# Pair blocks with both halves of the activations in one matmul, an earlier pool product and another block order in a two-layer decoder trunk

## The chip, the cores and the metric

The kernel runs on one core of one Trainium2 chip. The metric is the device time of one execution in microseconds (us), as the median of several runs. The kernel before takes 931.28 us (three runs, 930.87 to 931.46). The profile shows one execution on the same core.

## The reference, cut to what matters

Two layers are applied to a sequence of 256 tokens of width 1024, in float32. Each layer is a feed-forward, a mixer with three parallel head groups, and a second feed-forward; every sub-layer stands between two RMS norms.

```python
for l in range(2):
    f = swiglu(rmsnorm(h, ff1_norm_pre[l]), ff1_w_gate[l], ff1_w_up[l], ff1_w_down[l])   # 1024 -> 2816 -> 1024
    h = h + 0.5 * rmsnorm(f, ff1_norm_post[l])
    m = concat([ssd, pool, attention](rmsnorm(h, mix_norm_pre[l]) @ w_in[l])) @ w_out[l]
    h = h + rmsnorm(m, mix_norm_post[l])
    f = swiglu(rmsnorm(h, ff2_norm_pre[l]), ff2_w_gate[l], ff2_w_up[l], ff2_w_down[l])
    h = h + 0.5 * rmsnorm(f, ff2_norm_post[l])
# swiglu(h, wg, wu, wd) = (silu(h @ wg) * (h @ wu)) @ wd
# pool: per group of 64 columns, (sliding mean of u - u) @ pool_w[g], times pool_scale
```

## The kernel before

**Numbers in two parts.** Every operand of a large product is split into a high part `hi`, which ScalarE rounds to the matmul's reduced float32 format, and a remainder `lo` = x - hi, which VectorE forms. A product is then hi·hi + hi·lo + lo·hi, three matmuls. The weights are split on the chip, as they arrive: class `Weights` (L49) loads a unit of 128 x 2048 numbers (1 MB) on the SyncE queue into one of four raw buffers, and `split_next` (L88) makes a job of it, of which at most five are held split at a time. `pump` (L116) loads and splits as far ahead as those buffers allow. The ScalarE rounding is L104, the VectorE remainder L105, and L103 is a sum or difference of two raw units that is wanted as a weight.

**A feed-forward** (`ffn`, L521) cuts the 2816 inner columns into eleven blocks of 256. The first two (`ffn_first`, L422) are computed as soon as the normed input is turned. Of the other nine, the list `QUADS` = 2, 5, 8 names where a *seven* begins and `PAIRS` = 4, 7, 10 the *pairs*:

- A seven (`ffn_quad`, L473) makes two neighbouring blocks, gate and up, for all tokens with seven products of half sizes in place of eight, by sums of the four weight units g1, u1, u2, g2 (jobs g1, T1, T2, T3, g2, T4, u2; each is `product`, L463, 12 matmuls of 512 columns). Its result is the two tiles `h0`, `h1`, which are finished by VectorE after the last products (L512 for h1, L515 for h0).
- A pair (`ffn_pair`, L449) makes one block's gate and its up with `mm_feat` (L313): for each of two groups of 128 output columns, 24 matmuls, where the weight is the stationary operand and 256 tokens of `xT` stream: 8 of hi·x_hi, 8 of hi·x_lo, 8 of lo·x_hi. The two groups share one PSUM bank; gate and up have a bank each. L417 takes the Silu from PSUM, L419 multiplies.

After a seven, its `h0` and `h1` have to be turned by eight transposes (`turn_h`, L446) before its down products. The next block calls that as `turn()`: a pair between its gate and its up (L456), a seven behind its first product (L481). The down products (`mm_rows`, L358) go to four `acc` banks, two for each half of the tokens (t = 0, 1), 12 matmuls for a block and half. Those of the last four blocks are done for t = 0 first, so that the closing norm of t = 0 (`post`, L239) and the opening norm of the next sub-layer (`pre_scale`, L255, whose last step is L260) run on ScalarE, VectorE and GpSimd while TensorE still works for t = 1. Then `pre_turn` (L263) turns the normed tile by transposes, L270.

**The mixer** (`mixer`, L614) ends with: the attention's product (`attend`), the second gate product `zed(1)`, the two scans (`scan`, L926) and the carry between them (L917), the pool product (L967, two matmuls on VectorE's `d`) with its scaling and split (`rows_out`, L869, L219, L220), and the output product: units wa, wp, ws0, ws1 of `w_out` through `mm_rows`, again into two acc banks for each half of the tokens. wa needs the attention, wp the pool, ws0 and ws1 the gated scan after its norm, which `gated_turn` (L944) turns. At the end of t = 1's ws1, `joint` puts the `pre_turn` of the t = 0 half between its two banks.

**Order.** The five engines run what the tile framework's scheduler made of the program; `tc.issue_after` lets a stretch be placed behind a named instruction. The order of each engine is fixed when the program is built. Four `wk` banks and four `acc` banks of PSUM are handed out in turn.

Of the kernel before, what the change touches and what calls it, by code (L numbers as in the profile page):

```python
# [11 lines left out]
F32R = mybir.dt.float32r  # L12
BF16 = mybir.dt.bfloat16
AF = mybir.ActivationFunctionType
ALU = mybir.AluOpType
AX = mybir.AxisListType

P = 128
D = 1024
S = 256  # L20
NT = S // P
DEPTH = 2
KD = D // P
# [6 lines left out]
UNIT = 2048  # L30
# [2 lines left out]
SPLIT_BUFS = 5  # L33
TAIL = 4

FIRST, QUADS, PAIRS = (0, 1), (2, 5, 8), (4, 7, 10)


C_ID, C_U, C_SGT, C_NEG, C_CNT, C_CS = 0, 128, 256, 384, 512, 1024
# [101 lines left out]
def hybrid_trunk_kernel(ctx: ExitStack, tc: tile.TileContext, a, out: bass.AP):  # L141
# [16 lines left out]
    def bank(tag="wk"):  # L158
        return psum.tile([P, 512], F32, tag=tag, name=f"{tag}{next(ids)}")
# [47 lines left out]
        nc.scalar.activation(neg_b, cst[:, C_NEG : C_NEG + P], AF.Copy)  # L207

    gains = consts.tile([P, 2, D], F32, name="gains")
    xT = [consts.tile([P, KD, S], F32R, name=f"xT{i}") for i in range(2)]  # L210

    def load_gain(which, l, n):
        row = a["gains"][l, n : n + 1, :]
# [99 lines left out]
    def mm_feat(ps, u, c, x=xT, ncols=256):  # L313

        hi, lo = (w[:, : KD * ncols].rearrange("p (k n) -> p k n", k=KD) for w in W.get(u))
        s = slice(c, c + P)
        for i, (w, y) in enumerate(((hi, x[0]), (hi, x[1]), (lo, x[0]))):
            for k in range(KD):
                nc.tensor.matmul(ps, w[:, k, s], y[:, k, :], start=i == 0 and k == 0, stop=i == 2 and k == KD - 1)  # L319

    def mm_tok(ps, u, t, ncols=256):

        hi, lo = (w[:, : KD * ncols].rearrange("p (k n) -> p k n", k=KD) for w in W.get(u))
        s = slice(t * P, (t + 1) * P)
        for i, (x, w) in enumerate(((xT[0], hi), (xT[0], lo), (xT[1], hi))):
            for k in range(KD):
                nc.tensor.matmul(ps, x[:, k, s], w[:, k, :], start=i == 0 and k == 0, stop=i == 2 and k == KD - 1)  # L327
# [41 lines left out]
    def plan_ffn(l, n):  # L369


        p = {}

        def down(i):
            p["d", i] = W.plan(a[f"ff{n}_d"][l, i])

        def pair(i):
            for k in "gu":
                p[k, i] = W.plan(a[f"ff{n}_{k}"][l, PAIRS.index(i)])

        for i in range(2):
            for k in range(2):
                p["f", i, k] = W.plan(a[f"ff{n}_f"][l, 2 * i + k], pieces=4)
        before = list(FIRST)
        for i in range(2, NU):
            if i in PAIRS:
                pair(i)
                for b in before:
                    down(b)
                before = [i]  # L390
            elif i in QUADS:
                src = a[f"ff{n}_q"][l, QUADS.index(i)]
                g1, u1, u2 = (W.unit(src[k]) for k in (0, 1, 3))
                p["g1", i] = W.job(g1, pieces=2 if i > QUADS[0] else 4)
                p["T1", i] = W.job(g1, (g1, ALU.add, u1), then=(u1, src[3]))
                p["T2", i] = W.job(g1, (g1, ALU.add, u2))
                late = i == QUADS[-1]
                if not late:
                    down(before[0])
                p["T3", i] = W.job(u1, free=(u1,))  # L400
                g2 = W.unit(src[2])
                p["g2", i] = W.job(g2)
                for b in before[1:]:
                    down(b)
                p["T4", i] = W.job(g1, (g1, ALU.add, g2), free=(g1, g2))
                p["u2", i] = W.job(u2, free=(u2,))
                if late:
                    down(before[0])
                before = [i, i + 1]
        for b in before:  # L410
            down(b)
        return p

    def gate(pg, pu, s=None):
        if s is None:
            s = buf()
            nc.scalar.activation(s, pg, AF.Silu)  # L417
        hf = buf()
        nc.vector.tensor_tensor(hf, pu, s, op=ALU.mult)  # L419
        return hf  # L420
# [26 lines left out]
            split_into(hT[i], (slice(None), slice(None)), ps)  # L447

    def ffn_pair(i, p, turn):  # L449
        pg, pu = bank(), bank()  # L450
        for ps, k in ((pg, "g"), (pu, "u")):
            for j in range(2):
                mm_feat(ps[:, j * 256 : (j + 1) * 256], p[k, i], j * P)
            W.done(p[k, i])
            if k == "g":
                turn()  # L456
        hf = gate(pg, pu)
        hT = (buf(F32R), buf(F32R))
        split_into(hT, (slice(None), slice(None)), hf)
        W.pump()  # L460
        return hT
# [8 lines left out]
                             skip_group_check=not first)  # L470
        W.done(job)

    def ffn_quad(i, p, left, turn, downs):  # L473


        late = i == QUADS[-1]
        pa = bank()
        product(pa, left["X11"], p["g1", i], True)
        w2 = buf()
        nc.scalar.activation(w2, pa, AF.Copy)  # L480
        turn()  # L481
        pc = bank()
        product(pc, left["S1"], p["T1", i], True)
        h1 = buf()
        nc.scalar.activation(h1, pc, AF.Copy)
        if "rest" in left:
            with tc.issue_after(split_into.last.ins):
                left.pop("rest")()
                W.pump()
        else:  # L490
            W.pump()
        pb = bank()
        product(pb, left["S2"], p["T2", i], True)
        nc.vector.tensor_tensor(w2, pb, w2, op=ALU.add)
        nc.vector.tensor_tensor(pc, pc, w2, op=ALU.subtract)
        W.pump()
        if not late:
            downs[0]()
        pd = bank()
        product(pd, left["S3"], p["T3", i], True)  # L500
        nc.vector.tensor_tensor(pd, pd, w2, op=ALU.add)
        nc.vector.tensor_tensor(h1, h1, pd, op=ALU.subtract)  # L502
        W.pump()
        product(pa, left["X12"], p["g2", i], False)
        h0 = buf()
        nc.scalar.activation(h0, pa, AF.Silu)
        W.pump()
        for f in downs[1:]:
            f()
        product(pd, left["X22"], p["T4", i], False)  # L510
        nc.scalar.activation(w2, pd, AF.Silu)
        nc.vector.tensor_tensor(h1, h1, w2, op=ALU.mult)  # L512
        W.pump()
        product(pc, left["S4"], p["u2", i], False)
        nc.vector.tensor_tensor(h0, pc, h0, op=ALU.mult)  # L515
        W.pump()
        if late:
            downs[0]()
        return [h0, h1]

    def ffn(l, n, p, gain, turned, left, next_left, before_next, last, later=None):  # L521
# [19 lines left out]
                W.pump()  # L541

        before = list(FIRST)
        for i in range(2, NU):
            if i not in QUADS + PAIRS:
                continue
            if hf:
                for b in before:
                    hT[b] = (buf(F32R), buf(F32R))

            def turn():
                if hf:
                    turn_h(hf, [hT[b] for b in before])

            if i in PAIRS:
                hT[i] = ffn_pair(i, p, turn)
                for b in before:
                    both(b)
                hf, before = None, [i]
            else:  # L560
                hf = ffn_quad(i, p, left, turn, [lambda b=b: both(b) for b in before])
                before = [i, i + 1]
            if later and i in PAIRS:
                later()
                later = None
# [48 lines left out]
    def mixer(l, p, turned, next_left, before_next):  # L614
# [341 lines left out]
        with tc.issue_after(turn_x.last.ins):  # L956
            sz1 = zed(1)
        with tc.issue_after(zed.last.ins):
            y0 = scan(0)
            yn0 = gated(0, y0, sz0)  # L960
            carry()
            y1 = scan(1)

            pp = bank("acc")
            pw = vec[:, V_PW : V_PW + 256].rearrange("p (j n) -> p j n", j=2)
            for j in range(2):
                m = nc.tensor.matmul(pp[:, j * 256 : (j + 1) * 256], pw[:, j, :], d[:, j, :], start=True, stop=True)  # L967
            y_pool = rows_out(pp, vec[:, V_PS : V_PS + 2])
            yn1 = gated(1, y1, sz1)
        acc = [banks2(), banks2()]  # L970
        with tc.issue_after(m.ins):
            mm_rows(acc[0], p["wa"], 0, y_attn, True, False)
        m = mm_rows(acc[0], p["wp"], 0, y_pool, False, False)
        with tc.issue_after(m.ins):
# [112 lines left out]
def _layout(inp):  # L1087
# [16 lines left out]

        return x.reshape(DEPTH, 2, 4, P, 512).transpose(0, 1, 3, 2, 4).reshape(DEPTH, 2, P, UNIT)

    def quads(g, u):


        q = []  # L1110
        for i in QUADS:
            for h in range(2):
                for w in (g, u):
                    x = w[:, h * 512 : (h + 1) * 512, i * 256 : i * 256 + 512]
                    q.append(x.reshape(DEPTH, 4, P, 512).transpose(0, 2, 1, 3).reshape(DEPTH, P, UNIT))
        return np.stack(q, axis=1).reshape(DEPTH, len(QUADS), 4, P, UNIT)

    for n in (1, 2):
        g, u = f[f"ff{n}_w_gate"], f[f"ff{n}_w_up"]
        d[f"ff{n}_f"] = np.concatenate([half(g[:, :, :512]), half(u[:, :, :512])], axis=1)  # L1120
        d[f"ff{n}_g"] = cols(g)[:, PAIRS]
        d[f"ff{n}_u"] = cols(u)[:, PAIRS]
        d[f"ff{n}_q"] = quads(g, u)
        d[f"ff{n}_d"] = rows(f[f"ff{n}_w_down"])
    w = f["w_in"]
    z, x, B, C, dt, u, q, k, v = np.split(w, np.cumsum([512, 512, 256, 256, 8, 256, 256, 256]), axis=2)
# [37 lines left out]
```

## Time and profile before

| | |
|---|---|
| median of three runs | 931.28 us |
| profiled execution, its own time | 931.69 us |
| its span, from the first to the last instruction | 930.0 us |
| mean granted TensorE clock | 0.997 |
| TensorE matmul busy | 917.9 us, 99% |
| VectorE busy | 785.5 us, 84% |
| ScalarE busy | 584.2 us, 63% |
| first feed-forward, mixer, second feed-forward of layer 0 | about 0 to 189, 189 to 291, 291 to 467 us |

PE is TensorE's matmul, PEld its weight load, DVE VectorE, ACT ScalarE, POOL GpSimd, SP SyncE. A row of the timeline reads: start in us, duration in us, engine, line, operation, output <- inputs by the program's names, shape, count; in brackets the idle time ahead of it on its engine and what ended that. Rows with a count cover consecutive instructions, which overlap a little in their pipelines; the time of one in a run is the distance of starts over the count.

### The profile page before, as it was taken

What the parts mean: (1) busy time and instruction counts of PE and PEld (TensorE: products, weight loads), DVE (VectorE), ACT (ScalarE), POOL (GpSimd) and SP (SyncE); (2) the same over time, 40 slices, a digit from 0 to 9 for tenths busy, and PEclk for the clock granted to TensorE, in tenths of its full rate; (3) what the DMA queues carried; (4) which work ended last, traced back from release to release, by engine and by line L of the source; (5) the groups of instructions that cost most, each with busy time, mean ns of one, the idle gap of its engine ahead of it and who ended that gap; (6) DMA issues with size and microseconds to landing.
All of it is one profiled execution on the core that took longest, in us unless ns stands there. A gap on an engine that the chain in (4) does not pass through costs nothing.

```text
span 930.0 us, 13066 instructions
## 1 busy us (share of the span) xinstructions
PE 917.9 (99%) x5058; PEld 794.0 (85%) x5058; DVE 785.5 (84%) x1019; ACT 584.2 (63%) x931; POOL 30.1 (3%) x49
## 2 busy tenths in 40 slices
PE   7999999999999999999999999999999999999997
PEld 5889898989988888888888988898998888989895
DVE  6999999589868998988599989876989699989872
ACT  7665747478738665646566756556794567656641
POOL 0000000000001000000000000000000110000000
PEclk9999999999999999999999999999999999999999
DMA  8576958465434486848455968583834246868521
GB/s 325 153 274 201 386 157 314 179 215 194 181 109 173 103 304 190 318 135 305 148 181 156 342 171 289 165 315 110 297 104 172 72 145 185 319 203 270 188 101 45
DMA packets 28002, 190.54 MB, mean 205 GB/s; under 512 B 3106, under 2 KB 3362, under 8 KB 5924
## 3 DMA queue, kind: packets, MB, share of 16 engines
q1 hardware_dynamic: 26068, 176.87, 52.1%
q0 software_dynamic: 1728, 12.58, 7.5%
q8 instruction: 39, 0.64, 0.3%
q10 hardware_dynamic: 144, 0.26, 0.1%
q14 instruction: 23, 0.19, 0.1%
HBM read 188.65 MB, written 1.05 MB: 204 GB/s over the span
## 4 chain that ended last, share of the span: by engine, by line
PE 95%; issue 1%; DVE 1%; DMA 1%; ACT 1%; POOL 0%; DVEq 0%; POOLq 0%; SPq 0%; ACTq 0%
PE acc L358 29%; PE wk L469 25%; PE wk L319 21%; PE wk L340 14%; PE wk L446 2%; PE wk L327 1%; PE wk L270 1%; DMA raw<-in_ff_f 1%; DVE lo L105 0%; PE acc L677 0%; PE acc L747 0%; ACT hi L104 0%; ACT n L227 0%; PE acc L879 0%; PE wk L905 0%
## 5 line engine op out<-in xcount | busy, mean ns | idle before, releaser
L104 ACT ACTIVATE hi<-raw 128x1024 fp32r<-128x1024 f32 (+2 forms) x452 | 401.1, 938 | 176.9 <-DVE raw L103 44.6
L105 DVE TENSOR_TENSOR lo<-raw,hi 128x1024 fp32r<-128x1024 f32 (+2 forms) x452 | 467.1, 1079 | 51.5 <-ACT hi L104 50.2
L358 PE MATMUL acc<-hi,t 128*128 128x512 f32 x832 | 216.2, 391 | 0.5 <-DVE t L896 0.5
L358 PEld LDWEIGHTS acc<-hi,t 128*128 128x128 f32 x832 | 154.8, 188 | 32.7 <-DVE t L896 1.4
L319 PE MATMUL wk<-xT,hi 128*128 128x256 f32 x1088 | 143.4, 284 | 0.0
L319 PEld LDWEIGHTS wk<-xT,hi 128*128 128x128 f32 x1088 | 136.7, 191 | 1.7
L358 PE MATMUL acc<-lo,t 128*128 128x512 f32 x416 | 114.1, 390 | 0.0
L469 PE MATMUL wk<-hi,n 128*128 128x512 f32 x384 | 102.9, 390 | 0.0
L340 PE MATMUL wk<-hi,xT 128*128 128x512 f32 x384 | 99.0, 395 | 2.6 <-ACT hi L104 2.6
L358 PEld LDWEIGHTS acc<-lo,t 128*128 128x128 f32 x416 | 78.0, 188 | 16.2
L103 DVE TENSOR_TENSOR raw<-raw,raw 128x1024 f32<-128x1024 f32 x72 | 86.2, 1219 | 1.9 <-DMA raw<-in_ff_q 1.9
L340 PEld LDWEIGHTS wk<-hi,xT 128*128 128x128 f32 x384 | 71.6, 189 | 17.6 <-ACT hi L104 3.4
L469 PEld LDWEIGHTS wk<-hi,n 128*128 128x128 f32 x384 | 71.8, 188 | 14.7
L469 PE MATMUL wk<-hi,xT 128*128 128x512 f32 x288 | 77.8, 392 | 0.0
L319 PE MATMUL wk<-xT,lo 128*128 128x256 f32 x544 | 76.8, 283 | 0.0
L319 PEld LDWEIGHTS wk<-xT,lo 128*128 128x128 f32 x544 | 70.3, 192 | 0.0
L469 PEld LDWEIGHTS wk<-hi,xT 128*128 128x128 f32 x288 | 53.5, 188 | 12.6 <-DVE t L502 1.8
L340 PE MATMUL wk<-lo,xT 128*128 128x512 f32 x192 | 52.3, 395 | 0.0
L469 PE MATMUL wk<-lo,n 128*128 128x512 f32 x192 | 51.3, 389 | 0.0
L244 DVE TENSOR_TENSOR n<-acc,gains 128x512 f32<-128x512 f32 x24 | 16.1, 689 | 33.6 <-ACT n L227 33.6
L340 PEld LDWEIGHTS wk<-lo,xT 128*128 128x128 f32 x192 | 36.6, 191 | 7.8
L469 PEld LDWEIGHTS wk<-lo,n 128*128 128x128 f32 x192 | 36.0, 188 | 7.5
(175 smaller groups left out, 731.2 us busy)
## 6 DMA issues: line engine op xcount, KB each, us to landing
raw<-in_ff_q SPq DMA_DIRECT2D x48, 1024.0 KB, 5.0
raw<-in_ff_d SPq DMA_DIRECT2D x44, 1024.0 KB, 5.0
raw<-in_ff_f SPq DMA_DIRECT2D x16, 1024.0 KB, 6.2
raw<-in_ff_q POOLq DMA_DIRECT2D x12, 1024.0 KB, 8.0
raw<-in_ff_g SPq DMA_DIRECT2D x12, 1024.0 KB, 4.8
raw<-in_ff_u SPq DMA_DIRECT2D x12, 1024.0 KB, 4.9
raw<-in_w_in SPq DMA_DIRECT2D x10, 1024.0 KB, 4.8
raw<-in_w_kvz SPq DMA_DIRECT2D x8, 1024.0 KB, 5.0
```

What stands on the lines that cost most here:

```text
L103: nc.vector.tensor_tensor(raw[:, s], self.raw[x][:, s], self.raw[y][:, s], op=op)
L104: self.act = nc.scalar.activation(hi[:, s], raw[:, s], AF.Copy)
L105: nc.vector.tensor_tensor(lo[:, s], raw[:, s], hi[:, s].bitcast(F32), op=ALU.subtract)
L244: nc.vector.tensor_tensor(fg[i], f[i], gains[:, 1, i * 512 : (i + 1) * 512], op=ALU.mult)
L270: pre_turn.last = nc.tensor.transpose(ps[:, k * P : (k + 1) * P], xn[i][:, k * P : (k + 1) * P], ident)
L319: nc.tensor.matmul(ps, w[:, k, s], y[:, k, :], start=i == 0 and k == 0, stop=i == 2 and k == KD - 1)
L327: nc.tensor.matmul(ps, x[:, k, s], w[:, k, :], start=i == 0 and k == 0, stop=i == 2 and k == KD - 1)
L340: m = nc.tensor.matmul(ps, y[:, k, :], w[:, k, :], start=h == 0 and n == 0, stop=h == 1 and n == len(parts) - 1)
L358: m = nc.tensor.matmul(acc[b], x[:, j, s], w[:, j, b * 512 : (b + 1) * 512], start=first and j == 0 and i == 0, stop=last and j == 1 and i ...
L446: nc.tensor.transpose(ps[:, j * S + t * P : j * S + (t + 1) * P], hf[t][:, c], ident)
L469: nc.tensor.matmul(ps, x[:, k, :], w[:, k, :], start=first and n == 0, stop=n == len(parts) - 1, skip_group_check=not first)
```

## The change

Three edits stand together.

1. **Pairs side by side.** The two halves of the activations, `xT[0]` (high) and `xT[1]` (low), become the two halves of one tile `both`. A new `mm_side` streams x_hi and x_lo in one matmul of 512 columns against the high weight (8 for each group of 128 output columns), then 8 of 256 columns for lo·x_hi into the bank's second half. Each group has a bank of its own, and its two halves have to be added: ScalarE copies one half out, VectorE adds the other. `ffn_pair` takes its Silu and its product from SBUF.
2. **Pool product first.** In the mixer the pool product and its `rows_out` move ahead of the scans, and the wa product now follows the second scan.
3. **Order of the first feed-forward.** For layer 0, n = 1 alone, the sevens are blocks 3, 5, 8 and the pairs 2, 7, 10: pair, seven, seven, pair, seven, pair, where it was seven, pair, seven, pair, seven, pair. The weights are laid out for it on the host. `later`, which loads the constants, two gains and the mixer's parameters, is called behind the first pair, so now behind the first of these blocks instead of the second.

```diff
-FIRST, QUADS, PAIRS = (0, 1), (2, 5, 8), (4, 7, 10)
+FIRST = (0, 1)
+def blocks(l, n):
+    return ((3, 5, 8), (2, 7, 10)) if (l, n) == (0, 1) else ((2, 5, 8), (4, 7, 10))
...
-    xT = [consts.tile([P, KD, S], F32R, name=f"xT{i}") for i in range(2)]
+    both = consts.tile([P, 2, KD, S], F32R, name="xT")
+    xT = [both[:, i] for i in range(2)]
...
+    def mm_side(u, out):
+        hi, lo = (w[:, :UNIT].rearrange("p (k n) -> p k n", k=KD) for w in W.get(u))
+        for j in range(2):
+            s = slice(j * P, (j + 1) * P)
+            ps = bank()
+            for k in range(KD):
+                nc.tensor.matmul(ps, hi[:, k, s], both[:, :, k, :], start=k == 0, stop=k == KD - 1)
+            for k in range(KD):
+                nc.tensor.matmul(ps[:, S:], lo[:, k, s], xT[0][:, k, :], start=False, stop=k == KD - 1,
+                                 skip_group_check=True)
+            o = out[:, j * S : (j + 1) * S]
+            nc.scalar.activation(o, ps[:, S:], AF.Copy)
+            nc.vector.tensor_tensor(o, ps[:, :S], o, op=ALU.add)
+        W.done(u)
+        return out
...
     def ffn_pair(i, p, turn):
-        pg, pu = bank(), bank()
-        for ps, k in ((pg, "g"), (pu, "u")):
-            for j in range(2):
-                mm_feat(ps[:, j * 256 : (j + 1) * 256], p[k, i], j * P)
-            W.done(p[k, i])
-            if k == "g":
-                turn()
-        hf = gate(pg, pu)
+        s = mm_side(p["g", i], buf())
+        nc.scalar.activation(s, s, AF.Silu)
+        turn()
+        hf = mm_side(p["u", i], buf())
+        nc.vector.tensor_tensor(hf, hf, s, op=ALU.mult)
...
         with tc.issue_after(zed.last.ins):
+            pp = bank("acc")
+            pw = vec[:, V_PW : V_PW + 256].rearrange("p (j n) -> p j n", j=2)
+            for j in range(2):
+                pooled = nc.tensor.matmul(pp[:, j * 256 : (j + 1) * 256], pw[:, j, :], d[:, j, :], start=True, stop=True)
+            y_pool = rows_out(pp, vec[:, V_PS : V_PS + 2])
+        with tc.issue_after(pooled.ins):
             y0 = scan(0)
             yn0 = gated(0, y0, sz0)
             carry()
             y1 = scan(1)
-
-            pp = bank("acc")
...
             yn1 = gated(1, y1, sz1)
         acc = [banks2(), banks2()]
-        with tc.issue_after(m.ins):
+        with tc.issue_after(scan.last.ins):
             mm_rows(acc[0], p["wa"], 0, y_attn, True, False)
```

**What moves on the engines: TensorE where the first feed-forward's first seven ends.** The program before: the seven's last product (`wk_425`), then the pair's gate (`wk_656`), and behind that the transposes of `t_569` (h0) and `t_438` (h1).

```order
L469 MATMUL wk_425<-hi_526,n_446 128x512 x4
L319 MATMUL wk_656<-xT_108,hi_549 128x256 x5
L469 MATMUL wk_534<-hi_486,xT_108 128x512 x4
...
L319 MATMUL wk_656<-xT_108,lo_550 128x256 x8
L446 MATMUL wk_706<-ident,t_569 128x128
L446 MATMUL wk_706<-ident,t_438 128x128
```

The program after: the seven's last three jobs end with `wk_610`; then comes the next seven's first product (`wk_798`), and then the transposes of `t_741` (h0) and `t_623` (h1).

```order
L492 MATMUL wk_610<-hi_667,n_631 128x512 x4
L492 MATMUL wk_798<-hi_699,xT 128x512 x4
L492 MATMUL wk_798<-lo_700,xT 128x512 x4
L492 MATMUL wk_798<-hi_699,xT 128x512 x4
L472 MATMUL wk_813<-ident,t_741 128x128
L472 MATMUL wk_813<-ident,t_623 128x128
```

A pair's gate of 48 matmuls stood between the two; now one product of 12 does.

**VectorE at the same place.** L110 are the sums for a seven's jobs, L112 the remainders, L534 finishes h1, L537 makes h0 (`t_741`). The program before first (its L103, L105, L512, L515 are the same steps), then the program after.

```order
L105 TENSOR_TENSOR lo_550<-raw_469,hi_549 128x1024
L105 TENSOR_TENSOR lo_572<-raw_494,hi_571 128x1024 x2
L105 TENSOR_TENSOR lo_604<-raw_496,hi_603 128x1024 x2
L512 TENSOR_TENSOR t_438<-t_438,t_409 128x512
L515 TENSOR_TENSOR t_569<-wk_425,t_569 128x512
```

In the program after, `hi_720` and `hi_743` are the next seven's jobs T1 and T2, and `hi_765` is a down unit.

```order
L110 TENSOR_TENSOR raw_583<-raw_583,raw_648 128x1024 x2
L112 TENSOR_TENSOR lo_721<-raw_583,hi_720 128x1024 x2
L110 TENSOR_TENSOR raw_583<-raw_583,raw_650 128x1024 x2
L534 TENSOR_TENSOR t_623<-t_623,t_608 128x512
L112 TENSOR_TENSOR lo_744<-raw_583,hi_743 128x1024
L112 TENSOR_TENSOR lo_766<-raw_673,hi_765 128x1024
L112 TENSOR_TENSOR lo_744<-raw_583,hi_743 128x1024
L112 TENSOR_TENSOR lo_766<-raw_673,hi_765 128x1024
L537 TENSOR_TENSOR t_741<-wk_610,t_741 128x512
```

So the next seven's T1 and T2 and a down unit are prepared ahead of h0. On ScalarE, `hi_720` stands directly behind the Silu of the g2 product.

**TensorE where the mixer ends its t = 0 half.** The program before: the last matmul of t = 0 (`acc_2653`), the turn of the second gated half (`wk_2713`), t = 1's matmuls (`acc_2654`, `acc_2655`), and the transposes of the next sub-layer's input (`wk_2798`).

```order
L358 MATMUL acc_2653<-hi_2576,t_2470 128x512 x2
L944 MATMUL wk_2713<-ident,t_2650 128x128 x4
L358 MATMUL acc_2655<-lo_2296,t_2525 128x512
...
L358 MATMUL acc_2654<-hi_2576,t_2470 128x512 x2
L270 MATMUL wk_2798<-ident,n_2752 128x128 x4
```

The program after, with `acc_2586` for t = 0, `acc_2587` and `acc_2588` for t = 1:

```order
L383 MATMUL acc_2586<-hi_2509,t_2403 128x512 x2
L967 MATMUL wk_2646<-ident,t_2583 128x128 x4
L383 MATMUL acc_2588<-hi_2333,t_2533 128x512
...
L383 MATMUL acc_2587<-hi_2509,t_2403 128x512 x2
L278 MATMUL wk_2731<-ident,n_2685 128x128 x4
```

Between the turn of the gated half and the transposes of the input stood 35 matmuls of 512 columns; now 21 do, in both layers. The other 14, of wa and wp for t = 1, have moved ahead of ws0 for t = 0.

More of the change, by code (lines that the diff above doesn't have):

```diff
@@ L372, in plan_ffn @@
         p = {}
+        QUADS, PAIRS = blocks(l, n)
         def down(i):
@@ L471, in product, with ffn_quad @@
         W.done(job)
-    def ffn_quad(i, p, left, turn, downs):
-        late = i == QUADS[-1]
+    def ffn_quad(i, p, left, turn, downs, late):
         pa = bank()
@@ L543, in ffn @@
         before = list(FIRST)
+        QUADS, PAIRS = blocks(l, n)
         for i in range(2, NU):
@@ L560, in ffn @@
             else:
-                hf = ffn_quad(i, p, left, turn, [lambda b=b: both(b) for b in before])
+                hf = ffn_quad(i, p, left, turn, [lambda b=b: both(b) for b in before], i == QUADS[-1])
                 before = [i, i + 1]
@@ L962, in mixer @@
             y1 = scan(1)
-            pp = bank("acc")
[L965 to L968, printed above, removed]
             yn1 = gated(1, y1, sz1)
         acc = [banks2(), banks2()]
-        with tc.issue_after(m.ins):
+        with tc.issue_after(scan.last.ins):
             mm_rows(acc[0], p["wa"], 0, y_attn, True, False)
@@ L1105, in half, with quads, pairs @@
         return x.reshape(DEPTH, 2, 4, P, 512).transpose(0, 1, 3, 2, 4).reshape(DEPTH, 2, P, UNIT)
-    def quads(g, u):
+    def quads(g, u, n):
         q = []
[L1111 to L1116, printed above, removed]
+        for l in range(DEPTH):
+            for i in blocks(l, n)[0]:
+                for h in range(2):
+                    for w in (g, u):
+                        x = w[l, h * 512 : (h + 1) * 512, i * 256 : i * 256 + 512]
+                        q.append(x.reshape(4, P, 512).transpose(1, 0, 2).reshape(P, UNIT))
+        return np.stack(q).reshape(DEPTH, -1, 4, P, UNIT)
+    def pairs(w, n):
+        w = cols(w)
+        return np.stack([w[l, list(blocks(l, n)[1])] for l in range(DEPTH)])
     for n in (1, 2):
@@ L1120, in _layout @@
         d[f"ff{n}_f"] = np.concatenate([half(g[:, :, :512]), half(u[:, :, :512])], axis=1)
-        d[f"ff{n}_g"] = cols(g)[:, PAIRS]
-        d[f"ff{n}_u"] = cols(u)[:, PAIRS]
-        d[f"ff{n}_q"] = quads(g, u)
+        d[f"ff{n}_g"] = pairs(g, n)
+        d[f"ff{n}_u"] = pairs(u, n)
+        d[f"ff{n}_q"] = quads(g, u, n)
         d[f"ff{n}_d"] = rows(f[f"ff{n}_w_down"])
```

## Prediction

> **What bounds the kernel now.** I read the page first, then TensorE's own waits, then the chain of waits, then the timelines of three places.
>
> ```profile
> span 930.0 us, 13066 instructions
> PE 917.9 (99%) x5058; PEld 794.0 (85%) x5058; DVE 785.5 (84%) x1019; ACT 584.2 (63%) x931; POOL 30.1 (3%) x49
> ```
> ```profile
> PE wk L340 <- ACT hi L104: 2.6, 1, 2.6
> PE wk L199 <- DVE n L193: 2.3, 1, 2.3
> PE acc L358 <- DVE t L896: 0.5, 2, 0.3
> PE wk L270 <- DVE n L260: 0.5, 1, 0.5
> ```
>
> TensorE is the bound: it is busy 99%, and all its waits come to 5.9 us, nearly all at the start. So only two things change the time: what a matmul costs, and whether TensorE begins to wait where it doesn't now. The chain (start, duration, what) gives the cost of a matmul, at places where one row begins as the last one ends.
>
> ```profile
> 344.19 5.75 PE wk L319 x48
> 349.94 0.87 PE wk L446 x8
> ...
> 367.47 8.16 PE wk L469 x36
> ```
>
> A matmul of 256 columns takes 5.75 / 48 = 119.8 ns, one of 512 columns 8.16 / 36 = 226.7 ns. Two of 256 are 239.6 ns, so a matmul has a part of its own of about 12.9 ns that does not grow with its columns.
>
> **Edit 1, the matmuls of a pair: -4.9 us.** For gate or up, 48 matmuls of 256 columns become 16 of 512 and 16 of 256: 16 x 0.2267 + 16 x 0.1198 = 5.54 us instead of 5.75, so 0.21 less. There are 12 pairs with two such phases each: 24 x 0.206 = 4.9 us, all on the path. No row shows a matmul of 512 columns that reads its moving operand in two pieces. The bounds are that it costs like one of 512 (-4.9) or like two of 256 (0); I take the first, since the row of 512 is the same instruction but for the stride.
>
> [...]
>
> **Edit 1, the extra evictions: 0.** Each phase adds two copies of 128x256 on ScalarE and two adds on VectorE. The nearest rows:
>
> ```profile
> 273.77 0.39 ACT L219 ACTIVATE t<-wk 128x256 fp32r<-128x256 f32 x1 [0.72 <-PE wk L944]
> 274.45 0.42 DVE L220 TENSOR_TENSOR t<-wk,t 128x256 fp32r<-128x256 f32 x1
> ```
> ```profile
> 291.00:467.00 176.00, 176.00 (x937) 152.00 (x936) 151.79 (x167) 109.39 (x153) 5.75 (x7) 1.00 0.65 215
> ```
> ```profile
> 449.60 0.69 DVE L419 TENSOR_TENSOR t<-wk,t 128x512 f32<-128x512 f32 x1 [3.00 <-PE wk L319]
> 451.41 0.69 DVE L220 TENSOR_TENSOR t<-t,t 128x512 fp32r<-128x512 f32 x1
> ```
>
> 48 x 0.42 = 20 us more for VectorE and 48 x 0.39 = 19 us for ScalarE over the kernel, about 5 us in each feed-forward, where VectorE has 24 us idle in 176 (the first row is one feed-forward: behind its length stand the busy times of PE, PEld, DVE, ACT and POOL). After the last pair the way from the last matmul to the finished `hT` was 449.60 to 452.10, 2.5 us; with a copy, an add and two more split pieces (0.6 each) ahead it is some 4.5. The 24 down matmuls of blocks 8 and 9 for t = 0 (5.4 us) cover it. If that cover were gone it would cost up to 1 us in each feed-forward. Below zero nothing is to be had here.
>
> **Edit 3, the order of the first feed-forward: +4.0 us.** In the chain, the rows of TensorE follow one another from the first of these to the last, so the order has nothing to win.
>
> ```profile
> 24.13 0.87 PE wk L270 x8
> ...
> 73.39 0.87 PE wk L446 x8
> ...
> 189.43 0.87 PE wk L270 x8
> ```
> What it can lose lies where a seven now follows a seven. TensorE, between the end of the seven's g2 product and the transposes of h0, has T4, u2 and the next seven's g1: three products, 3 x 2.72 = 8.16 us. VectorE's and ScalarE's steps up to h0 run one behind another in a fixed order.
>
> ```profile
> 110.77 0.58 ACT L506 ACTIVATE t<-wk 128x512 f32<-128x512 f32 x1
> 111.32 2.02 ACT L104 ACTIVATE hi<-raw 128x1024 fp32r<-128x1024 f32 x2
> 96.33 1.06 ACT L104 ACTIVATE hi<-raw 128x1024 fp32r<-128x1024 f32 x1 [2.05 <-DMA raw<-in_ff_q]
> 30.64 2.36 DVE L103 TENSOR_TENSOR raw<-raw,raw 128x1024 f32<-128x1024 f32 x2
> 32.91 0.69 DVE L220 TENSOR_TENSOR n<-t,n 128x512 fp32r<-128x512 f32 x1
> 55.49 6.90 DVE L105 TENSOR_TENSOR lo<-raw,hi 128x1024 fp32r<-128x1024 f32 x6
> 62.30 0.70 DVE L501 TENSOR_TENSOR wk<-wk,t 128x512 f32<-128x512 f32 x1
> 70.31 0.69 DVE L512 TENSOR_TENSOR t<-t,t 128x512 f32<-128x512 f32 x1
> 70.91 0.69 DVE L515 TENSOR_TENSOR t<-wk,t 128x512 f32<-128x512 f32 x1
> 75.11 2.36 DVE L105 TENSOR_TENSOR lo<-raw,hi 128x1024 fp32r<-128x1024 f32 x2 [1.24 <-ACT hi L104]
> ```
>
> ScalarE takes the Silu of the g2 product (the next instruction starts 0.55 after it) and then the first half of T1's `hi`, 1.06. On VectorE follow two remainders, two sums, the step that finishes h1, four remainders and h0: eight of 1024 columns at (62.30 - 55.49) / 6 = 1.135 (the sums have the same: 2.27 for two), one at 0.60 and one of 0.69, together 10.37. With 0.3 for the three hand-overs (an estimate; 110.77 + 0.55 meets the next row within 0.01, hand-overs between engines are some 0.1) that is 0.55 + 1.06 + 10.37 + 0.3 = 12.3 against 8.16: TensorE waits about 4.0. Where this part starts doesn't matter, since both sides count from the same product. VectorE may come to it late on top, as it has no pause in this stretch now until 73.9 (75.11 - 1.24); and the hand-overs may be shorter: 3.5 to 5.5. The order before lost nothing at its seam: there a pair's gate (5.75) stood in between too, and at 70.91 + 0.69 h0 was in time for the transposes at 73.39.
>
> The constants and parameters that `later` loads are now queued on SyncE ahead of the second seven's u1. A landing takes 5 to 6 us (the last column):
>
> ```profile
> raw<-in_ff_q SPq DMA_DIRECT2D x48, 1024.0 KB, 5.0
> cst<-in_consts SPq DMA_DIRECT2D x1, 544.0 KB, 5.9
> ```
>
> By the order, u1's buffer only comes free behind the first seven's T4 sums, so its load could not start much earlier without them; I take 0, at most 1 us.
>
> **Edit 2, the pool product first: -1.1 us where it was, +5.3 us behind it.** First the place that it leaves.
>
> ```profile
> 268.05 1.07 PE L358 MATMUL acc<-hi,t 128*128 128x512 f32 x4
> 269.37 2.11 PE L358 MATMUL acc<-hi,t 128*128 128x512 f32 x8 [0.25 <-DVE t L896]
> 271.32 1.07 PE L358 MATMUL acc<-lo,t 128*128 128x512 f32 x4
> ```
>
> Twelve matmuls from 268.05 to 271.32 take 3.27 instead of 12 x 0.2267 = 2.72: 0.55 lost while a bank of the carry is still read. With the pool product ahead, that bank is wanted 12 matmuls later. Two layers: -1.1 (0 to -1.1). The pool's own evictions (two scalings, a copy, a remainder) now run ahead of the scans' on ScalarE and VectorE, some 0.6 us later for `gated`, whose turn has 24 matmuls of cover.
>
> Then what moved with it. The scheduler has put 14 matmuls of t = 1 ahead of the end of t = 0, so that they no longer stand behind it. The closing norm of t = 0 and the opening norm after it begin with the last matmul of t = 0.
>
> ```profile
> 279.79 0.60 PE L944 MATMUL wk<-ident,t 128*128 128x128 f32 x4
> 288.18 1.03 PE L270 MATMUL wk<-ident,n 128*128 128x128 f32 x8
> ```
> ```profile
> 286.62 1.42 DVE L260 SCALAR_TENSOR_TENSOR n<-h,s,gains 128x512 f32<-128x512 f32 x2 [0.44 <-POOL s L232]
> ```
> ```profile
> 735.06 0.60 PE L944 MATMUL wk<-ident,t 128*128 128x128 f32 x4
> 743.45 1.03 PE L270 MATMUL wk<-ident,n 128*128 128x128 f32 x8
> ```
>
> From the end of t = 0 (279.79) the normed tile is ready at 286.62 + 1.42, that is 8.25 later. TensorE came to the transposes after 8.39, and to the second four, which need the second half of the tile, after 8.39 + 0.44 = 8.83 (eight transposes take 0.87): the chain was hidden with some 0.52 to spare (0.06 for the hand-over), in both layers (735.06 to 743.45 is 8.39 as well). Now 14 x 0.2267 = 3.17 of that cover is gone, so TensorE waits 3.17 - 0.52 = 2.65, twice: +5.3 (4.5 to 6.0; shorter if the chain drops one of the split pieces that ScalarE has in between, longer by as much if it takes one up).
>
> **The sum.** -4.9 + 4.0 - 1.1 + 5.3 = +3.3 us. Against the profiled execution's 931.69 us that is 935.0; the median of the runs is 0.4 lower, so I forecast 934.6 us, 0.36% slower. A measurement of this kernel can tell about 0.2% (1.9 us) from no change.
>
> **The rivals.**
>
> - *The norm chain keeps up (faster).* If in the mixers the way from the last matmul of t = 0 to the normed tile fell from 8.25 to under 5.7 us, the transposes would not be late, and 934.6 - 5.3 = 929.3 would come out. For it: four split pieces of 512 columns (half of the 0.96 to 1.06 above) stand on ScalarE inside the chain and could go elsewhere. Against it: without all four it is still 8.25 - 2.0 = 6.2, and as built they are there. Chance 0.12.
> - *The seam of the two sevens hides.* If h0 is ready when the 12 matmuls are done, 934.6 - 4.0 = 930.6, no difference that can be told. It needs VectorE's order to be other than built, or its work to be a third cheaper. Chance 0.14.
> - *The fixed part of a matmul isn't saved.* If the two-piece read costs like two matmuls, the first term is 0: 939.5. The row of 512 speaks against it, no row for it. Chance 0.08. [...]
> - *VectorE falls behind in a feed-forward* by its 5 us more, and T4's products wait on its sums: +1 to +3, 935.6 to 937.6. Inside the range; chance 0.10.
>
> My forecast has the rest, 0.56.
>
> **How the numbers follow.** The low end takes in the hidden seam: 930.4. The high end has the upper bounds of the waits (5.5, 6.0) with the late VectorE: 934.6 + 1.5 + 0.7 + 2 = 938.8, cut to 938.4. Left out are the first rival and the third, 0.20 together. Faster by over 0.2% is the first rival, 0.12; within 0.2% the second, 0.14; slower the others, 0.74.
>
> **What would show it.** In the profile after: the 16 matmuls of 512 in a phase at 226.7 ns each (step 1; 240 refutes it); a wait of TensorE of 3.5 to 5.5 us near 87 us, on VectorE's h0, ahead of `turn_h` (edit 3); waits of about 2.6 us ahead of `pre_turn` at the end of both mixers, on the last step of `pre_scale` (edit 2), and none on the carry's bank. TensorE's waits, 5.9 us now, should come to about 15. If they stay near 6, the last two terms are wrong and the kernel is faster.

## The result, and the profile after

The changed kernel takes 940.0 us (median of 4 runs, 938.78 to 941.16) against 931.08 before (930.83 to 931.46): ratio 1.0095, 95% interval 1.0078 to 1.0113. It is slower, as forecast, but by 8.9 us where 3.5 were forecast, and outside the range. The profiled execution has a span of 939.4 us in 941.16.

The page, and then TensorE's waits (total, number of times, longest):

```profile
span 939.4 us, 12404 instructions
PE 918.9 (98%) x4674; PEld 777.6 (83%) x4674; DVE 802.3 (85%) x1067; ACT 602.6 (64%) x979; POOL 31.7 (3%) x49
```
```profile
PE wk L278 <- DVE n L268: 5.6, 3, 2.5
PE wk L472 <- DVE t L537: 4.1, 1, 4.1
PE wk L206 <- DVE n L200: 2.3, 1, 2.3
PE wk L365 <- ACT hi L111: 2.0, 1, 2.0
```

The waits are those of the forecast, almost to the tenth: 4.1 ahead of `turn_h` on h0 (4.0 said), 2.5 at the end of each mixer (2.65 said), none left on the carry's bank, 14.0 in all (about 15 said). The matmuls of a pair are too. The chain of waits in a pair's phase:

```profile
352.55 1.81 PE wk L336 x8
354.36 0.95 PE wk L338 x8
355.31 1.84 PE wk L336 x8
357.15 0.96 PE wk L338 x8
```

Eight matmuls of 512 columns in two pieces take 1.81 to 1.84, so 226 to 230 ns each, and the phase 5.56 instead of 5.75. What was not forecast stands in TensorE's busy time: 384 matmuls fewer, and yet it is busy 918.9 us instead of 917.9. Some matmuls have become slower. The chain behind the seam shows which:

```profile
90.47 1.19 PE wk L472 x8
91.65 6.93 PE wk L492 x24
98.58 5.44 PE acc L383 x24
```

Twenty-four matmuls of 512 take 5.44 us in the next row (5.44 to 5.54 in the chain's other rows of 24); right behind the wait they take 6.93, and the eight transposes 1.19 where the next ones need 0.87. It is the first eight of the 24 that are slow: they start from 91.31 on and the ninth at 94.79, 435 ns apiece. The granted clock (the fifth number of a row of TensorE by stretches, after the stretch, its length, the busy time and the count) is half there:

```profile
87.70:91.11 3.41, 0.65 (x6) 1.00 0.31 48
91.11:94.52 3.41, 3.41 (x12) 0.52 0.88 312
94.52:97.93 3.41, 3.41 (x16) 0.98 0.60 255
292.49:295.90 3.41, 1.28 (x9) 1.00 0.60 195
295.90:299.31 3.41, 3.41 (x10) 0.52 0.29 118
299.31:302.72 3.41, 3.41 (x16) 0.98 0.44 132
749.90:753.31 3.41, 1.03 (x8) 1.00 0.51 183
753.31:756.72 3.41, 3.41 (x11) 0.52 0.30 127
```

Behind each of the three new waits TensorE gets half its clock for 3.41 us (0.52, since the stretches of this table miss its bounds by a little) and does 10 to 12 matmuls where it does 16. The trace's records of the clock say 0.5 for 3.413 us each time, from 91.27, 296.07 and 753.45 us on, and once behind the start, from 12.76 us on. These four lie 23, 60 and 134 times 3.413 us apart.

The trace of before held the sign. Its longest wait, 2.6 us, stands near its start (it ends at 11.89 us), and the stretch around and behind it reads:

```profile
10.00:20.00 10.00, 8.08 (x27) 0.83 0.91 356
```

### The profile page after: what moved, and what is told of

Same layout as the page of the kernel before. It is cut to its first block, busy times and chain, and to the rows that moved or that the text cites. A ratio compares the mean times of both kernels' runs of the same rounds, so it can differ in the third digit from the quotient of the medians.

```text
span 939.4 us, 12404 instructions
## 1 busy us (share of the span) xinstructions
PE 918.9 (98%) x4674; PEld 777.6 (83%) x4674; DVE 802.3 (85%) x1067; ACT 602.6 (64%) x979; POOL 31.7 (3%) x49
## 4 chain that ended last, share of the span: by engine, by line
PE 87%; DVE 5%; issue 3%; ACT 2%; DMA 2%; POOL 0%; DVEq 0%; POOLq 0%; ACTq 0%
PE acc L383 25%; PE wk L492 21%; PE wk L365 14%; PE wk L336 9%; PE wk L327 6%; PE wk L338 4%; DVE lo L112 3%; PE wk L472 1%; DMA raw<-in_ff_d 1%; PE wk L352 1%; PE wk L278 1%; ACT hi L111 1%; PE wk L949 1%; ACT n L235 1%; DVE raw L110 1%
## 5 line engine op out<-in xcount | busy, mean ns | idle before, releaser
L112 DVE TENSOR_TENSOR lo<-raw,hi 128x1024 fp32r<-128x1024 f32 (+2 forms) x452 | 467.6, 1077 | 48.2 <-ACT hi L111 40.7
L336 PE MATMUL wk<-xT,hi 128*128 128x512 f32 x384 | 96.7, 394 | 0.0
L110 DVE TENSOR_TENSOR raw<-raw,raw 128x1024 f32<-128x1024 f32 x72 | 87.0, 1217 | 4.4 <-DMA raw<-in_ff_q 4.4
L336 PEld LDWEIGHTS wk<-xT,hi 128*128 128x128 f32 x384 | 69.7, 189 | 12.9
L338 PEld LDWEIGHTS wk<-xT,lo 128*128 128x128 f32 x384 | 52.4, 190 | 3.7
L338 PE MATMUL wk<-xT,lo 128*128 128x256 f32 x384 | 53.6, 282 | 0.0
```

The source lines that it names most:

```text
L110: nc.vector.tensor_tensor(raw[:, s], self.raw[x][:, s], self.raw[y][:, s], op=op)
L112: nc.vector.tensor_tensor(lo[:, s], raw[:, s], hi[:, s].bitcast(F32), op=ALU.subtract)
L336: nc.tensor.matmul(ps, hi[:, k, s], both[:, :, k, :], start=k == 0, stop=k == KD - 1)
L338: nc.tensor.matmul(ps[:, S:], lo[:, k, s], xT[0][:, k, :], start=False, stop=k == KD - 1, skip_group_check=True)
```

## The experiments

Theory A: the missing 5 us are the clock. A wait costs its own length, and from some length on about 1.6 us of half clock too. Rival B: a wait costs its length alone, and the rest comes from elsewhere: the pairs' saving that does not come through, VectorE or transfers. Later a second question came up, about VectorE (A2).

**One edit at a time.** `e1_pairs_only` is the kernel before with `mm_side`, `both` and the new `ffn_pair` alone. `e2_old_blocks` and `e3_old_pool` are the changed kernel with one part undone, `e7_blocks_only` is the kernel before with the new `blocks` alone:

```
e2:
-    return ((3, 5, 8), (2, 7, 10)) if (l, n) == (0, 1) else ((2, 5, 8), (4, 7, 10))
+    return (2, 5, 8), (4, 7, 10)
e3:
-        with tc.issue_after(zed.last.ins):
-            pp = bank("acc")
...
+            y1 = scan(1)
+            pp = bank("acc")
```

> The kernel before with edit 1 alone (pairs side by side). Theory A (the 5 us that the prediction lacks are the clock: after each of the three new waits TensorE is granted half its clock for 3.4 us): none of the waits is here, so only the matmuls of the pairs change, 24 phases at 0.18 to 0.2 us, 4.3 to 4.9 us: 926.2 to 926.8 us, and no half clock behind the start. Rival B (the pairs do not save what they should, because the extra evictions make TensorE wait in small pieces): 929 to 932 us.

> The changed kernel with the old order of blocks in the first feed-forward. Theory A: the wait at the seam goes (a gap of 4.5 us where a matmul takes 0.23, so 4.3) and with it one stretch of half clock (1.3 to 1.7): 940.0 - 5.8 = 934.2 us. Rival B (waits cost their length alone): 940.0 - 4.3 = 935.7 us.

> The changed kernel with the old place of the pool product. Theory A: two waits of 2.66 go and two stretches of half clock (1.65 and 1.9 in the trace), the wait on the carry's bank comes back (0.55 in each layer): 940.0 - 5.3 - 3.5 + 1.1 = 932.3 us. Rival B: 940.0 - 5.3 + 1.1 = 935.8 us.

> The kernel before with the new order of blocks in the first feed-forward alone. Theory A: a wait of some 4.1 us on h0 at the seam of the two sevens and one stretch of half clock behind it, 931 + 4.1 + 1.6 = 936.7 us; without the clock 935.1 us. Rival (the seam only waits because the pairs side by side have put VectorE behind): 931 to 933 us.

Measured: e1 928.87 us (ratio 0.9976, 0.9967 to 0.9985), e2 936.48 (1.0065, 1.0054 to 1.0077), e3 932.31 (1.0014, 1.0006 to 1.0023), e7 937.35 (1.0066, 1.0052 to 1.0079), beside 930.81 and 931.01 of the kernel before. As differences of medians:

| edit | in company of | cost |
|---|---|---|
| pairs | old order of blocks (e1 - before) | -1.9 |
| pairs | new order of blocks (e3 - e7) | -5.0 |
| blocks | pairs as before (e7 - before) | +6.3 |
| blocks | pairs side by side (after - e2; e3 - e1) | +3.5; +3.4 |
| pool | old order of blocks, pairs side by side (e2 - e1) | +7.6 |
| pool | both others (after - e3) | +7.7 |

From before by e7 and e3 to after: 6.3 - 5.0 + 7.7 = 9.0, the whole. Pool came out as A had it (7.7), and so did e7 (936.7 expected, 937.35 measured). e1 came out 2.1 to 2.7 us higher than A expected, near the low end of what rival B gave, and e2 (936.48, with waits of 1.3 and 1.0 us at the same lines) lies 2.3 above A's 934.2 and 0.8 above B's. These two alone do not speak for A. The waits of e1 tell what A left out; VectorE's timeline there stands behind them, and then that of before at the same steps (L516 is L494 there, L517 is L495):

```profile
PE wk L492 <- DVE t L524: 1.1, 1, 1.1
PE wk L492 <- DVE wk L517: 0.7, 1, 0.7
```
```profile
145.50 5.76 DVE L112 TENSOR_TENSOR lo<-raw,hi 128x1024 fp32r<-128x1024 f32 x5
151.18 0.68 DVE L516 TENSOR_TENSOR t<-wk,t 128x512 f32<-128x512 f32 x1
...
152.92 0.69 DVE L517 TENSOR_TENSOR wk<-wk,t 128x512 f32<-128x512 f32 x1
```
```profile
148.26 0.69 DVE L494 TENSOR_TENSOR t<-wk,t 128x512 f32<-128x512 f32 x1
...
149.99 0.70 DVE L495 TENSOR_TENSOR wk<-wk,t 128x512 f32<-128x512 f32 x1
```

With pairs side by side and the old order VectorE comes to these steps 2.9 us later than before, at the third seven of the first feed-forward, and the products that add to those banks wait. I read it so: VectorE's own work per seven is long, a pair is where it catches up, and the pair is now shorter for TensorE and longer for VectorE.

e2 leaves something open. Its six executions had granted clocks from 0.992 to 0.997. Two stretches of half clock, with the 0.8 us that half clock costs the changed kernel's profile at its end (half from 937.77 us to the end at 939.4; 1.0 in the profile before), would give 0.996 or less; yet the two at 0.997 took 936.08 and 936.41 us, hardly less than the three at 0.993 to 0.995 (936.45 to 936.80). So the +7.6 of its row can't be read as the price of two such stretches.

**VectorE's part (A2).** `e6_pool_adds` moves the added sums to GpSimd, `e8_first_plain` leaves the first feed-forward's three pairs as they were:

```
e6:
+            q = buf()[:, :S]
             nc.scalar.activation(o, ps[:, S:], AF.Copy)
-            nc.vector.tensor_tensor(o, ps[:, :S], o, op=ALU.add)
+            nc.scalar.activation(q, ps[:, :S], AF.Copy)
+            nc.gpsimd.tensor_tensor(o, q, o, op=ALU.add)
e8:
-                hT[i] = ffn_pair(i, p, turn)
+                hT[i] = ffn_pair(i, p, turn, (l, n) == (0, 1))
```

> Pairs side by side alone, with the added sums of a pair on GpSimd (ScalarE copies both halves, GpSimd adds them) instead of VectorE. Theory A2 (with pairs alone VectorE falls behind in the first feed-forward, and the two waits of 0.7 and 1.1 us near 153 us are its price): VectorE has 5 us less in each feed-forward, the waits there go, 926.5 to 927.2 us. Rival (those waits have another cause, such as transfers, or GpSimd is slower and its result late): 928.9 us or more.

> Pairs side by side alone, but the three pairs of the very first feed-forward as before. Theory A2: 6 phases lose their 0.18 (1.1 us), the waits of 1.8 near 153 us go: 928.9 + 1.1 - 1.8 = 928.2 us, and a granted clock that is the same in every run. Rival (the waits are not VectorE's): 930.0 us.

Measured: e6 927.72 (0.9967, 0.9954 to 0.9979), e8 927.2 (0.9958, 0.9945 to 0.997). In e8 nothing is left of the waits near 153 us; these are all of TensorE's waits:

```profile
PE wk L206 <- DVE n L200: 2.3, 1, 2.3
PE wk L365 <- ACT hi L111: 2.2, 1, 2.2
PE wk L278 <- DVE n L268: 0.6, 1, 0.6
PE acc L383 <- DVE t L932: 0.5, 2, 0.3
```

In e6 1.1 us in three small waits remain, the longest, 0.6, at 108 us, and the time is 0.5 us over what was expected. So the waits near 153 us were VectorE's. e8 beats both kernels, by 0.42% (3.8 us) against before, which is 18 of the 24 phases at the forecast 0.206 (3.7). That is 1.0 us less than A2 expected: the pairs of the first feed-forward cost more in e1 than the 1.8 us of waits that its profile shows, and the rest is open.

**The clock by itself.** `e4_filled` leaves the waits and gives TensorE unused matmuls to do in them:

```
+    def fill(ps, n):
+        for k in range(n):
+            m = nc.tensor.matmul(ps, both[:, 0, 0, :P], both[:, 0, 2 * (k % 4) : 2 * (k % 4) + 2, :], start=True, stop=True)
+            if idle and not i:
+                with tc.issue_after(idle.ins):
+                    fill(ps, 16)
```

> The changed kernel with matmuls that nobody uses in the three waits (16 of 512 columns at the seam, 3.6 us; 10 at the end of each mixer, 2.3 us), into the bank that the next transposes overwrite; nothing comes later by them. Theory A: the real work waits as long as before, but TensorE keeps its full clock: 940.0 - 4.9 = 935.1 us, half clock only at the start, and TensorE's waits fall to some 6 us. Rival B (the slower matmuls behind a wait have another cause than TensorE's idleness, such as transfers or VectorE): 940 us, still three stretches of half clock.

Measured: 936.58 us (1.0063, 1.0051 to 1.0075), 3.4 below the changed kernel. The same places by stretches:

```profile
91.11:94.52 3.41, 3.41 (x19) 1.00 0.98 339
...
293.41:296.82 3.41, 3.31 (x18) 1.00 0.52 221
```

Matmuls whose results nobody uses made the kernel faster; no length of a wait can explain that, and B falls. Of the expected 4.9 us 1.5 are missing. In the profile of e4 a wait of 1.3 us on VectorE stands at 570 us that the changed kernel does not have, behind a transfer that took 6.76 us in the chain; why it comes there was not tried.

**A shorter wait.** `e10_short_wait` takes split pieces out of ScalarE's way inside the norm chain at the mixer's end:

```
         xn1 = before_next(1)
-        W.pump(SPLIT_BUFS - 1)
+        W.pump(2)
+        with tc.issue_after(normed.ins):
+            W.pump(SPLIT_BUFS - 1)
```

> The changed kernel with the split pieces of the next stage's later units queued on ScalarE behind the opening norm instead of inside it; TensorE's order is the same row for row. The normed tile is some 1.1 us earlier, so the wait of 2.5 us at the end of each mixer falls to 1.0 to 1.6. Theory A (a wait costs its length, and from some 2 us on a stretch of half clock too): the two stretches there go as well, 940.0 - 2 x (1.1 + 1.75) = 934.3 us. Rival B (a wait costs its length alone): 940.0 - 2.2 = 937.8 us.

Measured: 934.49 us (1.0036, 1.0024 to 1.0049). The timeline of TensorE there:

```profile
292.86 1.38 PE L278 MATMUL wk<-ident,n 128*128 128x128 f32 x8 [0.85 <-DVE n L268]
...
295.46 1.07 PE L365 MATMUL wk<-hi,xT 128*128 128x512 f32 x4
```

The waits fell from 2.50 to 0.85, 3.3 us for both; the kernel became 5.5 us faster. The other 2.2 us go with the two stretches of half clock: the granted clock is 0.995 in the profiled execution and 0.992 in the changed kernel's (two such stretches are 0.004 of it), and the first four matmuls of the next stage, the second row, take 1.07 there. In the changed kernel they take 1.77:

```profile
294.52 1.38 PE L278 MATMUL wk<-ident,n 128*128 128x128 f32 x8 [2.50 <-DVE n L268]
...
298.00 1.77 PE L365 MATMUL wk<-hi,xT 128*128 128x512 f32 x4
```

**How long a wait may be.** `e5_dose` and `e11_dose_fine` put twelve waits of different lengths into the kernel before:

```
+        nc.scalar.activation(d[0], src, AF.Copy)
+        n = next(doses)
+        for k in range(n):
+            nc.gpsimd.tensor_copy(d[(k + 1) % 2], d[k % 2])
+        tc.keep_in_program_order(nc.tensor.transpose(ps[:, :P], d[n % 2][:, :P], ident))
```

> The kernel before, with a wait of its own between gate and up of each of the 12 pairs: ScalarE copies the gate's bank, GpSimd copies the tile on 0, 3, 1, 4, 2, 5, 1, 3, 2, 6, 0, 4 times, and TensorE transposes a part of the last copy into the bank that up overwrites. Nothing is left out. Theory A (idle time of TensorE itself takes its clock away): waits from about 2.5 us on are each followed by one stretch of half clock of 3.4 us, waits under 1.5 us by none, whatever stands behind them; the time is 931 us plus the waits plus 1.65 us for each such stretch. Rival B (the slow matmuls belong to the places where they were seen, transposes with a loaded VectorE behind them): no half clock at these places, or at all of them.

> As the kernel with 12 added waits, but with 1 and 2 copies on GpSimd by turns, so that the waits lie between 1 and 4.5 us. [...] Rival C (a fixed length decides): all waits over one length lose the clock and none under it.

Measured: 995.72 and 978.84 us, one run each. Some of the waits, from TensorE's timelines (the bracket has the wait), of e5 and of e11:

```profile
420.83 0.48 PE L458 MATMUL wk<-ident,t 128*128 128x128 f32 x1 [3.40 <-POOL t L457]
671.75 0.33 PE L458 MATMUL wk<-ident,t 128*128 128x128 f32 x1 [0.99 <-POOL t L457]
964.59 0.33 PE L458 MATMUL wk<-ident,t 128*128 128x128 f32 x1 [2.34 <-POOL t L457]
```
```profile
74.15 0.33 PE L458 MATMUL wk<-ident,t 128*128 128x128 f32 x1 [1.36 <-POOL t L457]
416.57 0.33 PE L458 MATMUL wk<-ident,t 128*128 128x128 f32 x1 [1.85 <-POOL t L457]
555.15 0.33 PE L458 MATMUL wk<-ident,t 128*128 128x128 f32 x1 [3.20 <-POOL t L457]
```

And e11 by stretches behind the last two of these:

```profile
416.60:420.00 3.40, 3.40 (x17) 0.53 0.65 92
...
555.20:558.60 3.40, 3.40 (x30) 1.00 0.27 111
```

Where TensorE kept its clock behind a wait, the 16 matmuls of 256 that follow the transposes took 2.15 us; where it lost it, 3.01 to 3.76 (where the timeline stops before the 16th, 141 to 154 ns for each against 218 to 258). A wait of 1.85 us lost the clock (twice, at 416 and 897 us: 3.01 and 3.67), one of 3.20 did not (2.15). So no fixed length decides, and rival C falls; what does decide between such waits was not shown. Of the 24 waits of e5 and e11 the nine of 0.69 to 1.36 us and those of 2.34 and 3.20 kept the clock; the two of 1.85, that of 3.13 and the ten of 3.40 to 9.17 lost it. That the places do it, rival B of e5, falls with these two kernels: at the sixth pair a wait of 4.03 us lost the clock in e5 (3.76) and one of 0.99 kept it in e11 (2.15).

One stretch for each long wait, as A had it for e5, did not hold. Seven waits there were of 3.1 us or more, so A gives 931 + 43.2 (all twelve waits) + 7 x 1.65 = 985.8 us, and it took 995.72. The granted clock of 0.974 over the span of 994.0 us says the same: it is worth some 52 us at half clock, about 15 stretches of 3.413 us (an estimate from these two numbers), of which the start and the end have some 1.6 in the kernel before (3.41 and 2.02 us) and A has seven behind the waits.

## Why the prediction was wrong

- *What bounds the kernel*: right, TensorE. But "only two things change the time" left out the third, what clock TensorE is granted, although the stretch behind the start showed 0.83.
- *Edit 1, the matmuls*: right. -5.0 (e3 against e7) for the forecast -4.9. The rival that the fixed part is not saved fell, though its 939.5 lies near the result: the matmuls take 226 to 230 ns, not 240.
- *Edit 1, the evictions*: 0 held in the changed kernel and failed beside the old order, where about 3 us are taken back, 1.8 of them in the two waits on VectorE. I looked for its cost after the last pair, where it is covered; it showed at the third seven's sums. That 0 came true in the changed kernel was luck: edit 3 happened to spare what edit 1 costs. The rival that VectorE falls behind is true of pairs alone.
- *Edit 3*: the wait was right, and by its reason: 4.1 for 4.0, and VectorE's steps up to h0 run from 79.94 to 90.31 us in the trace after, the forecast 10.37. "The order has nothing to win" was not. Alone the order costs 6.3, the wait and the half clock behind it; beside edit 1 it costs 3.5, since it spares VectorE's 2 to 3 us at the third seven. That the long wait at the seam is where VectorE catches up is argued from the waits that are gone, not shown.
- *Edit 2*: waits right (2.50 for 2.65, none on the carry), price wrong: 7.7 for 4.2.
- *The step that failed* is the one from wait to time: "so TensorE waits 3.17 - 0.52 = 2.65, twice: +5.3", and the +4.0 of edit 3 likewise. Each wait was priced at its length; e4, e10 and the doses show the half clock on top. Going from before by e7 and e3 to the changed kernel, the terms came out at +6.3 for +4.0, -5.0 for -4.9 and +7.7 for +4.2, together 5.7 us more; three stretches at half clock are 5.1 (half of 3 x 3.413). How much of it they are in the medians is less sure: e4 saves 3.4 us, with a new wait of 1.3 in its profiled execution, and e10 shows 1.1 for each stretch, where half of a record of 3.413 is 1.7. That part of a stretch falls into the wait itself is not the reason: in the profiled execution of the changed kernel all three begin 0.8 to 1.6 us behind the end of their waits (91.27 behind 90.47, 296.07 behind 294.52, 753.45 behind 752.18). The difference stays open.

## What to carry to other kernels

On a kernel whose TensorE is busy 99%, price a new wait of TensorE from 1.85 us on, the shortest that lost the clock in e5 and e11 (2.34 and 3.20 kept it there), at its length plus 1.1 (e10) to 1.7 us (half of a record of 3.413), and at more if it is as long as the seven of e5, and read the granted clock right behind the waits that the trace already has before you price the next one. Two edits that load the same second engine need not add: here the pairs were worth 1.9 or 5.0 us by the order of the blocks, so test each with and without the other. If a wait cannot be removed, make it as short as those that kept the clock here (0.69 to 1.36 us in e5 and e11, 0.85 in e10), or let TensorE do unused matmuls in it, as e4 did (3.4 us faster).

## What the runs showed of the hardware

- TensorE's matmuls were slow (in the changed kernel at a granted clock of 0.50, in e11 behind the first 1.85 us at 0.53) behind waits of 4.12 and twice 2.50 us (the changed kernel), twice 1.85 us (e11), 3.13 us (e5) and all ten of 3.40 to 9.17 us (e5, e11), and not behind nine of 0.69 to 1.36 us (e5, e11), one of 2.34 (e5) and one of 3.20 (e11).
- In the changed kernel each of these stretches of half clock lasted 3.413 us. In e5 there was more than one for a long wait: about 15 in all (the estimate above, from 0.974 over 994.0 us) beside seven waits of 3.1 us or more. Behind its waits of 7.60 and 9.17 us already the eight transposes took 1.91 us, where they took 1.04 behind the waits of 0.69 to 0.99.
- A moving operand of 512 columns in two pieces of 256 costs what one piece does: 226 to 230 ns in the changed kernel, beside 226.7 in the kernel before.
